# A fused encoder layer: the first input tile and the first weight tile loaded in halves, the norm weight alone in front of them

## The chip, the cores and the metric

The kernel runs on one core of a Trainium2 chip. The metric is the device time of one execution in microseconds; of several executions the median is given. A profile is one further execution recorded by the hardware profiler. Its times are counted from the first instruction, and its span is the time from the first to the last instruction.

## The reference

One layer of a hybrid encoder on an input of 512 positions by 1024 channels, in float32. The input is normalised, and one projection makes the inputs of three token mixers and the logits of three branch gates:

```python
h = rms_norm(x, norm_mix[l])                      # x * rsqrt(mean(x*x) + EPS) * g
proj = jnp.einsum('bsd,dc->bsc', h, w_in[l])      # 1024 -> 8192 columns
u_pool, u_lru, q, k, v, g_logits = jnp.split(proj, splits, axis=-1)
gates = jax.nn.sigmoid(g_logits + b_gate[l]).reshape(B, S, N_BRANCH, D_MODEL)
...
merged = (gates[:, :, 0] * (y_pool @ w_branch[l, 0])
          + gates[:, :, 1] * (y_lru @ w_branch[l, 1])
          + gates[:, :, 2] * (y_sb @ w_branch[l, 2]))
x = x + merged @ w_out[l]
h2 = rms_norm(x, norm_ffn[l])
x = x + (silu(h2 @ w_ffn_gate[l]) * (h2 @ w_ffn_up[l])) @ w_ffn_down[l]
```

`y_pool` comes from causal means over 2, 4, 8 and 16 positions, `y_lru` from a short convolution and a gated linear recurrence, `y_sb` from causal stick-breaking attention with 8 heads of 128. Of all this the change touches only the first step: the products of `norm_mix * x` with the first 512 gate columns of `w_in` (columns 5120 to 5631). The factor `rsqrt(mean(x*x) + EPS)` depends on the position alone and is multiplied in later.

## The kernel before, in words

**Precision.** Every operand of a large product is split into a high part, rounded to the matrix format (`fp32r`), and a low part, what the rounding left. A product then takes three matrix products: high by high, low weight by high input, high weight by low input. In the code `wh`/`wl` or `hi0`/`lo0` are the parts of a weight tile and `hh`/`hl` those of an input tile.

**Layout.** Channels lie on the 128 partitions, positions along the free dimension. The transposed input `xt` has 8 tiles of 128 x 512, numbered k. The small vectors of the layer (norm weights, biases, convolution taps, 114 columns in all) are packed in one array `vecs`, which a single transfer loads into the tile `vt` (L447). `vcol(name, i)` (L294) picks a column of it.

**The first stage.** Before any data is there, TensorE runs `WARM` = 9 products of a constant tile into a scratch bank (L421). Then the first four output tiles of the gate projection (4 x 128 columns, four accumulators) are computed k by k (L696): for each k, 4 products of `wh` by `hh`, 4 of `wl` by `hh`, 4 of `wh` by `hl`, each over 512 positions, 12 products a k and 96 in all. The weights come in chunks of two k (`("first", 0)` to `("first", 3)`). The first chunk is loaded and split by hand at L443 to L453: a transfer for each k, then a cast to `hi0` and a subtraction to `lo0` on VectorE. Later chunks go through `add_direct` and `split_w`: a transfer of 512 KB on SP (L117), the high part on ScalarE (L110), the low part on VectorE (L111). `make_h` (L433) makes `hh` of an input tile on ScalarE (L437: times the norm weight of that k) and `hl` on VectorE (L438). At k = 3 the loads and squares for the mean square are emitted (`input_rms`, L474).

**What sets the order.** Transfers are issued from SP's queue, in this stage also one from ScalarE's, and software transfers from POOL's. A planner assigns each engine its instruction order from the dependences, its own cost estimates and the order of the text; `tc.high_priority` moves blocks forward. So the order of the text is not always the order on the engine: the constants of the recurrence (`lru_constants`, L539 to L560: `qg`, the `lt` chain, `cpos`, `cneg`), which the text emits after the first chunks of the projection, run on VectorE as soon as `vt` is there. POOL computes one power of that chain (L547). Tiles have fixed places in SBUF; `pad` (L299, `PAD` columns) shifts what is allocated behind it.

**After it** come the other gate columns, the recurrence, the attention, the branch and output projections and the feed-forward network. From the attention projections on, many products are arranged as a seven-product scheme over halves of 256 columns (`product`, L282).

Of the kernel before, what the change touches and what calls it, by code (L numbers as in the profile page):

```python
# [8 lines left out]
F32 = mybir.dt.float32  # L9
F32R = mybir.dt.float32r  # L10
BF16 = mybir.dt.bfloat16
AF = mybir.ActivationFunctionType
ALU = mybir.AluOpType
# [3 lines left out]
P = 128  # L17
S = 512
D = 1024
KT = D // P  # L20
# [4 lines left out]
HD = 128  # L25
QSCALE = float(HD) ** -0.5
EARLY = 300
WARM = 9
GBUFS = 27
NDIRECT = 2  # L30
KD = 8
H = S // 2
AHEAD = 200
PAD = 41


OFF = 16
# [11 lines left out]
VOFF = {}  # L49
# [17 lines left out]
def layer_kernel(ctx: ExitStack, tc: tile.TileContext, x, xt, vecs, w_in, w_qkv7, w_gate7, w_pool, w_rg, w_ig,  # L67
                 w_branch, w_br7, w_out, w_fg, w_fu, w_fd, w_fd7, out):
    nc = tc.nc
    act = nc.scalar.activation  # L70
    dve = nc.vector

    cst = ctx.enter_context(tc.tile_pool(name="cst", bufs=1))
# [18 lines left out]
    def cols(ap, k0, nk, c0, nc_):  # L92
        return ap[k0 * P:(k0 + nk) * P, c0:c0 + nc_].rearrange("(k p) c -> p k c", p=P)
# [200 lines left out]
    def vcol(name, i=0):  # L294
        o = VOFF[name] + i
        return vt[:, o:o + 1]


    cst.tile([P, PAD], F32, tag="pad", name="pad")  # L299
    warm = cst.tile([P, S], BF16, tag="warm", name="warm")  # L300
    dve.memset(warm, 1.0)
# [106 lines left out]
    with ExitStack() as first:  # L408
# [18 lines left out]
        xts = [xp[k // 2][:, k % 2, :] for k in range(KT)]  # L427
        hu = []

        def load_xt(k):  # L430
            nc.sync.dma_start(xts[k], xt[k * P:(k + 1) * P, :])

        def make_h(k):  # L433
            t = t4([2, S], f"hu{k}", F32R)
            hh, hl = t[:, 0, :], t[:, 1, :]
            gcol = vcol("norm_mix", k)
            act(hh, xts[k], AF.Copy, scale=gcol)  # L437
            dve.scalar_tensor_tensor(hl, xts[k], gcol, hh.bitcast(F32), ALU.mult, ALU.subtract)  # L438
            hu.append((hh, hl))


# [1 line left out]
        hi0, lo0 = (t.rearrange("p (a b) -> p a b", a=2) for t in weight_tiles("whi0", "wlo0"))  # L443
        raw0 = wp.tile([P, 2, 512], F32, tag="raw", name="raw0")
        ready["first", 0] = hi0, lo0
        src0 = cols(w_in, 0, 2, 5120, 512)
        nc.sync.dma_start(vt, vecs)  # L447
        for k in range(2):
            load_xt(k)
            (nc.sync if k else nc.scalar).dma_start(raw0[:, k, :], src0[:, k, :])  # L450
            dve.tensor_copy(hi0[:, k, :], raw0[:, k, :])
            dve.tensor_tensor(lo0[:, k, :], raw0[:, k, :], hi0[:, k, :].bitcast(F32), ALU.subtract)
            make_h(k)  # L453
        load_xt(2)
        emit_next()
        make_h(2)
# [238 lines left out]
        pss = [chunk_psum(("gate", 0, c), pb) for c in range(2)]  # L695
        for k in range(KT):  # L696
            if k % 2 == 0:
                wh, wl = weights("first", k // 2)
            for w, x_ in ((wh, 0), (wl, 0), (wh, 1)):
                for n in range(4):  # L700
                    nc.tensor.matmul(pss[n // 2][n % 2], w[:, k % 2, n * P:(n + 1) * P], hu[k][x_],  # L701
                                     start=k == 0 and w is wh and x_ == 0,
                                     stop=k == KT - 1 and x_ == 1)
            if k == 3:
                input_rms()
        bg.append(rms_broadcast)
# [146 lines left out]
        for cc in range(2):  # L853
# [14 lines left out]
            for nm in ORDER:  # L868
                ps, half, first_, t, ts_, src, ss = plan[nm]
# [314 lines left out]
    with ExitStack() as third:  # L1184
# [42 lines left out]
        for u, nm in BORDER:  # L1227
            z, half, first_, sn, ts_ = plan[nm]
# [5 lines left out]
            for w in range(2):  # L1234
                o = ps[:, w, half * H:(half + 1) * H]
                for k in range(4):
                    for n, (x_, y_) in enumerate(((0, 0), (0, 1), (1, 0))):
                        nc.tensor.matmul(o, ah[x_][:, w, k, :], b[k][y_], start=first_ and n == k == 0,  # L1238
                                         stop=n == 2 and k == 3, skip_group_check=True)
            if sn is not None:  # L1240
                if (u, sn) not in snaps:
                    snaps[u, sn] = ap2.tile([P, 2, S], F32, tag="t", name=f"bt{u}{sn}")
                with tc.high_priority(EARLY):
                    act(snaps[u, sn][:, :, ts_], ps[:, :, hi], AF.Copy,
                        scale=-1.0 if sn and (u, sn) in gated else 1.0)
# [10 lines left out]
    with ExitStack() as ffn:  # L1256
# [18 lines left out]
        for c in range(4):  # L1275
# [7 lines left out]
            pss = psh[c] if c < 2 else chan_chunk(("out", c), mt, pool=fp)  # L1283
            hh = g4([2, S], f"h2h{c}", F32R)
            hl = g4([2, S], f"h2l{c}", F32R)
            for j in range(2):
                k = 2 * c + j
# [382 lines left out]
```

## Time and profile before

| what | value |
|---|---|
| median of 3 runs | 901.01 us (900.60 to 901.17) |
| the profiled execution | 900.73 us |
| its span | 899.0 us |
| TensorE busy | 893.4 us, 99% of the span |
| VectorE busy | 732.3 us, 81% |
| ScalarE busy | 523.2 us, 58% |
| granted clock of TensorE, mean | 1.000 |

In the rows of the profile PE is TensorE, PEld its weight loads, DVE VectorE, ACT ScalarE, POOL GpSimd, SP SyncE; a q behind the name is the engine's queue, where transfers are issued. A timeline row has start, length, engine, line, operation, output<-inputs and shape, and a count where neighbouring instructions are merged; in brackets stands how long the engine had been idle before and what ended that. The line is that of the kernel's source.

### The profile page before, as it was taken

The page shows a single profiled execution, that of the slowest core. Times are in us where ns is not written, and L with a number is a line of the kernel's source. Part 1 is how long each engine was busy: PE and PEld are TensorE (multiplying, and loading weights), DVE is VectorE, ACT ScalarE, POOL GpSimd, SP SyncE. Part 2 cuts the span into 40 slices and gives each one's busy share as a digit, 9 for nine tenths or more (in the row PEclk, how much of TensorE's full clock was granted, in tenths as well). Part 3 has the DMA queues.
Part 4 walks back from the last instruction along what each step waited for, and adds up shares of the span by engine and source line. Part 5 has one row for each costly group of instructions (what it writes and reads, how often), then busy time and mean ns, then how long its engine had stood idle before and what let it go on. Part 6 is the DMA issues. An engine that isn't in the chain of part 4 may idle for free.

```text
span 899.0 us, 14052 instructions
## 1 busy us (share of the span) xinstructions
PE 893.4 (99%) x5491; PEld 794.2 (88%) x5491; DVE 732.3 (81%) x922; ACT 523.2 (58%) x722; POOL 86.3 (10%) x126
## 2 busy tenths in 40 slices
PE   9999999999999999999999999999999999999998
PEld 6888778788899888888888988889999999989998
DVE  7897897988786599967887696699888888799764
ACT  7554989556856556555664544454555555664532
POOL 1110002232332101000001100000000000101200
PEclk9999999999999999999999999999999999999999
DMA  9585347789682785734736865245543333866842
GB/s 337 147 303 156 115 127 215 234 286 242 181 260 71 233 235 190 220 118 141 223 91 152 184 177 170 94 131 152 141 117 95 111 102 125 225 167 122 180 99 94
DMA packets 116579, 151.98 MB, mean 169 GB/s; under 512 B 8096, under 2 KB 90016, under 8 KB 116512
## 3 DMA queue, kind: packets, MB, share of 16 engines
q1 hardware_dynamic: 104416, 107.30, 37.7%
q0 software_dynamic: 11952, 43.52, 20.6%
q8 instruction: 43, 0.70, 0.3%
q10 hardware_dynamic: 144, 0.26, 0.1%
q14 instruction: 24, 0.20, 0.1%
HBM read 130.61 MB, written 18.87 MB: 166 GB/s over the span
## 4 chain that ended last, share of the span: by engine, by line
PE 95%; DVE 2%; ACT 2%; issue 1%; DMA 0%; SPq 0%; DVEq 0%; ACTq 0%
PE ps_y L287 11%; PE ps_x L287 8%; PE ps_q L798 7%; PE ps_dy L287 5%; PE ps_dx L287 4%; PE ps_br L278 3%; PE ps_br L279 3%; PE ps_br L280 3%; PE ps_gate L701 2%; PE ps_bY L1238 2%; PE ps_gy L287 2%; PE ps_gate L280 2%; PE ps_bX L1238 2%; PE ps_gx L287 2%; PE ps_gate L279 2%; PE ps_gate L278 2%
## 5 line engine op out<-in xcount | busy, mean ns | idle before, releaser
L110 ACT ACTIVATE whi<-raw 128x1024 fp32r<-128x1024 f32 x73 | 77.2, 1058 | 85.3 <-PE ps_out L279 17.0
L111 DVE TENSOR_TENSOR wlo<-raw,whi 128x1024 fp32r<-128x1024 f32 x73 | 89.1, 1220 | 32.9 <-ACT whi L110 32.9
L111 DVE TENSOR_TENSOR wlo<-qw,whi 128x1024 fp32r<-128x1024 f32 x48 | 58.6, 1222 | 20.8 <-ACT whi L110 20.5
L110 ACT ACTIVATE whi<-qw 128x1024 fp32r<-128x1024 f32 x48 | 50.8, 1057 | 33.1 <-PE ps_q L798 18.6
L1403 ACT ACTIVATE wh_S<-w_S 128x1024 fp32r<-128x1024 f32 x36 | 38.2, 1064 | 35.5 <-PE ps_y L287 22.4
L1404 DVE TENSOR_TENSOR wl_S<-w_S,wh_S 128x1024 fp32r<-128x1024 f32 x36 | 43.8, 1220 | 6.2 <-ACT wh_S L1403 6.2
L1403 ACT ACTIVATE wh<-w 128x1024 fp32r<-128x1024 f32 x27 | 28.8, 1066 | 30.3 <-issue 11.9
L1494 POOL DMA_DIRECT2D dw<-in_w_down_dram x16 | 13.5, 846 | 325.9 <-DVE wl L1404 248.2
L1404 DVE TENSOR_TENSOR wl<-w,wh 128x1024 fp32r<-128x1024 f32 x27 | 32.9, 1220 | 10.0 <-ACT wh L1403 10.0
L1403 ACT ACTIVATE whdS<-dw 128x1024 fp32r<-128x1024 f32 x16 | 17.0, 1064 | 24.4 <-PE ps_dy L287 13.2
L1404 DVE TENSOR_TENSOR wldS<-dw,whdS 128x1024 fp32r<-128x1024 f32 x16 | 19.6, 1224 | 12.9 <-ACT whdS L1403 12.9
L1054 DVE TENSOR_TENSOR_SCAN E<-K,ahead 128x512 f32<-128x512 f32 (+3 forms) x32 | 25.3, 812 | 4.4 <-ACT K L1050 4.4
L278 PE MATMUL ps_br<-yHH,whi 128*128 128x512 f32 x64 | 25.3, 395 | 0.0
L278 PE MATMUL ps_lru<-HH,whi 128*128 128x512 f32 x64 | 25.2, 394 | 0.0
L278 PE MATMUL ps_br<-yph,whi 128*128 128x512 f32 x64 | 25.2, 394 | 0.0
L278 PE MATMUL ps_pool<-HH,whi 128*128 128x512 f32 x64 | 25.2, 393 | 0.0
L279 PE MATMUL ps_br<-ypl,whi 128*128 128x512 f32 x64 | 25.0, 391 | 0.0
L280 PE MATMUL ps_gate<-HH,wlo 128*128 128x512 f32 x64 | 25.0, 391 | 0.0
L278 PE MATMUL ps_gate<-HH,whi 128*128 128x512 f32 x64 | 25.0, 391 | 0.0
L280 PE MATMUL ps_br<-yph,wlo 128*128 128x512 f32 x64 | 25.0, 391 | 0.0
L279 PE MATMUL ps_br<-yHL,whi 128*128 128x512 f32 x64 | 25.0, 390 | 0.0
L279 PE MATMUL ps_pool<-HL,whi 128*128 128x512 f32 x64 | 25.0, 390 | 0.0
(717 smaller groups left out, 3426.3 us busy)
## 6 DMA issues: line engine op xcount, KB each, us to landing
raw<-in_w_in_dram SPq DMA_DIRECT2D x31, 512.0 KB, 5.2
qw<-in_w_qkv_dram SPq DMA_DIRECT2D x24, 512.0 KB, 6.8
w<-in_w_ffn_gate_dram SPq DMA_DIRECT2D x36, 256.0 KB, 4.1
w<-in_w_ffn_up_dram SPq DMA_DIRECT2D x36, 256.0 KB, 4.6
raw<-in_w_branch_dram SPq DMA_DIRECT2D x16, 512.0 KB, 4.4
dw<-in_w_down_dram POOLq DMA_DIRECT2D x16, 512.0 KB, 6.3
qw<-in_w_qkv_dram POOLq DMA_DIRECT2D x12, 512.0 KB, 7.6
qd<-r POOLq DMA_DIRECT2D x12, 512.0 KB, 7.2
```

Source lines behind the costliest of these rows:

```text
L110: act(hi, raw, AF.Copy)
L111: dve.tensor_tensor(lo, raw, hi.bitcast(F32), ALU.subtract)
L278: nc.tensor.matmul(ps, lh, rh, start=start, stop=False, skip_group_check=skip)
L279: nc.tensor.matmul(ps, lh, rl, start=False, stop=False, skip_group_check=skip)
L280: nc.tensor.matmul(ps, ll, rh, start=False, stop=stop, skip_group_check=skip)
L287: nc.tensor.matmul(o, a_[a][:, w, k, :], b_[b][:, k, :], start=first and n == k == 0, stop=last and n == 2 and k == 3, skip_group_check=True)
L701: nc.tensor.matmul(pss[n // 2][n % 2], w[:, k % 2, n * P:(n + 1) * P], hu[k][x_], start=k == 0 and w is wh and x_ == 0, stop=k == KT - 1 a ...
L798: nc.tensor.matmul(ps[:, a, :], b_[:, k, ts_], a_[:, kk, :], start=first and n == k == 0, stop=n == 2 and k == 3, skip_group_check=True)
L1054: dve.tensor_tensor_scan(E[:, c0:c0 + n][:, ::-1], K[:, c0 + 1:c0 + n + 1][:, ::-1], ahead[:, S - n:][:, ::-1], 0.0, ALU.mult, ALU.add)
L1238: nc.tensor.matmul(o, ah[x_][:, w, k, :], b[k][y_], start=first_ and n == k == 0, stop=n == 2 and k == 3, skip_group_check=True)
L1403: act(h, src, AF.Copy)
L1404: dve.tensor_tensor(l, src, h.bitcast(F32), ALU.subtract)
```

## The change

- The norm weight's 8 columns get a tile of their own, `nmix`, loaded from `vecs` as the first transfer on SP; `make_h` takes its column from there. The pad shrinks from 41 to 33 columns.
- The first input tile is loaded as two transfers of 256 positions, the first on SP, the second on ScalarE's queue. The k = 0 part of the first weight tile is loaded as two transfers of 256 columns, the first on ScalarE's queue, the second on SP. The input tile of k = 1 and the k = 1 weight part follow on SP, and `vt` behind them.
- For k = 0, `hi0` and `lo0` are made in halves of 256 columns, and `hh` and `hl` in halves of 256 positions: both `hh` halves, then both `hl` halves.
- For k = 0 the products run in four groups: output tiles 0 and 1 with the first half of the positions, 0 and 1 with the second, 2 and 3 with the first, 2 and 3 with the second. Each group has 6 products of 256 positions, so 24 stand where 12 of 512 stood.
- `WARM` goes from 9 to 7.

```diff
-WARM = 9
+WARM = 7
-PAD = 41
+PAD = 33
...
+    nmix = cst.tile([P, 8], F32, tag="nmix", name="nmix")
...
-        def make_h(k):
+        def make_h(k, parts=(slice(0, S),)):
             t = t4([2, S], f"hu{k}", F32R)
             hh, hl = t[:, 0, :], t[:, 1, :]
-            gcol = vcol("norm_mix", k)
-            act(hh, xts[k], AF.Copy, scale=gcol)
-            dve.scalar_tensor_tensor(hl, xts[k], gcol, hh.bitcast(F32), ALU.mult, ALU.subtract)
+            gcol = nmix[:, k:k + 1]
+            for ts_ in parts:
+                act(hh[:, ts_], xts[k][:, ts_], AF.Copy, scale=gcol)
+            for ts_ in parts:
+                dve.scalar_tensor_tensor(hl[:, ts_], xts[k][:, ts_], gcol, hh[:, ts_].bitcast(F32),
+                                         ALU.mult, ALU.subtract)
             hu.append((hh, hl))
...
+        o = VOFF["norm_mix"]
+        nc.sync.dma_start(nmix, vecs[:, o:o + 8])
+
+        def round_first(k, cs):
+            dve.tensor_copy(hi0[:, k, cs], raw0[:, k, cs])
+            dve.tensor_tensor(lo0[:, k, cs], raw0[:, k, cs], hi0[:, k, cs].bitcast(F32), ALU.subtract)
+
+        HF = (slice(0, S // 2), slice(S // 2, S))
+        nc.scalar.dma_start(raw0[:, 0, HF[0]], src0[:, 0, HF[0]])
+        nc.sync.dma_start(xts[0][:, HF[0]], xt[0:P, HF[0]])
+        nc.scalar.dma_start(xts[0][:, HF[1]], xt[0:P, HF[1]])
+        nc.sync.dma_start(raw0[:, 0, HF[1]], src0[:, 0, HF[1]])
+        load_xt(1)
+        nc.sync.dma_start(raw0[:, 1, :], src0[:, 1, :])
+        for cs in HF:
+            round_first(0, cs)
+        make_h(0, HF)
+        round_first(1, slice(0, S))
+        make_h(1)
         nc.sync.dma_start(vt, vecs)
-        for k in range(2):
-            load_xt(k)
-            (nc.sync if k else nc.scalar).dma_start(raw0[:, k, :], src0[:, k, :])
-            dve.tensor_copy(hi0[:, k, :], raw0[:, k, :])
-            dve.tensor_tensor(lo0[:, k, :], raw0[:, k, :], hi0[:, k, :].bitcast(F32), ALU.subtract)
-            make_h(k)
...
-            for w, x_ in ((wh, 0), (wl, 0), (wh, 1)):
-                for n in range(4):
-                    nc.tensor.matmul(pss[n // 2][n % 2], w[:, k % 2, n * P:(n + 1) * P], hu[k][x_],
-                                     start=k == 0 and w is wh and x_ == 0,
-                                     stop=k == KT - 1 and x_ == 1)
+            for ns, ts_ in [(ns, ts_) for ns in ((0, 1), (2, 3)) for ts_ in HF] if k == 0 else \
+                    (((0, 1, 2, 3), slice(0, S)),):
+                for w, x_ in ((wh, 0), (wl, 0), (wh, 1)):
+                    for n in ns:
+                        nc.tensor.matmul(pss[n // 2][n % 2][:, ts_], w[:, k % 2, n * P:(n + 1) * P],
+                                         hu[k][x_][:, ts_],
+                                         start=k == 0 and w is wh and x_ == 0 and ts_ == HF[0],
+                                         stop=k == KT - 1 and x_ == 1, skip_group_check=True)
```

## The prediction

> **What bounds the kernel now.** I read the page's first part, then the chain of waits over the first 40 us, then the list of TensorE's own waits, and last the timelines of the first 12 us, engine by engine. The page says how much there is to win at all:
>
> ```profile
> span 899.0 us, 14052 instructions
> PE 893.4 (99%) x5491; PEld 794.2 (88%) x5491; DVE 732.3 (81%) x922; ACT 523.2 (58%) x722; POOL 86.3 (10%) x126
> ```
>
> TensorE is busy in all but 899.0 - 893.4 = 5.6 us of the span. The chain of waits in order of time (start, length, what) shows where a part of that lies:
>
> ```profile
> 0.74 0.39 SPq L447
> 1.19 3.35 DMA xt<-in_xt_dram
> 4.62 0.73 ACT hu L437
> 5.39 22.10 PE ps_gate L701 x96
> 27.49 0.23 PE ps_gate L278
> ```
>
> Behind the start stands one transfer (the first input tile), one activation that makes `hh` of it, and then 96 products without a break: 22.10 / 96 = 0.230 us each. So the first product starts at 5.39 and everything after it hangs on TensorE. TensorE's waits (engine, line, who ended it: total, times, longest):
>
> ```profile
> PE warm_ps L422 <- DVE warm L301: 1.5, 1, 1.5
> PE ps_gate L701 <- ACT hu L437: 0.5, 1, 0.5
> PE ps_q L798 <- DVE wlo L111: 0.4, 1, 0.4
> ```
>
> The third comes much later, and there are no others. A product begun earlier therefore moves the end by nearly as much, provided that the next tiles keep up.
>
> **What feeds the first products.** Transfers issued around 1.2 us, with the time from issue to landing; the second raw half of the first weight tile; the next weight chunk (512 KB); and a transfer with rows of 32 bytes:
>
> ```profile
> raw<-in_w_in_dram ACTq DMA_DIRECT2D x1, 256.0 KB, 3.1
> xt<-in_xt_dram SPq DMA_DIRECT2D x1, 256.0 KB, 3.3
> vt<-in_vecs_dram SPq DMA_DIRECT2D x1, 57.0 KB, 2.9
> ```
> ```profile
> raw<-in_w_in_dram SPq DMA_DIRECT2D x1, 256.0 KB, 4.5
> bigx<-in_vecs_dram SPq DMA_DIRECT2D x2, 2.0 KB, 6.8
> ```
> ```profile
> raw<-in_w_in_dram SPq DMA_DIRECT2D x1, 512.0 KB, 5.9
> ```
>
> SP's issues of interest (start, length over all, count), and what the transfer engines did, in windows whose last two columns are their busy share and GB/s:
>
> ```profile
> 1.19 0.90 SPq L431 DMA_DIRECT2D xt<-in_xt_dram  x2
> 2.12 0.43 SPq L450 DMA_DIRECT2D raw<-in_w_in_dram  x1
> 3.07 0.56 SPq L117 DMA_DIRECT2D raw<-in_w_in_dram  x1
> ```
> ```profile
> 0.00:5.00 5.00, 3.41 (x9) 1.14 (x9) 1.82 (x7) 1.97 (x3) 2.24 (x26) 1.00 0.66 189
> 5.00:10.00 5.00, 4.61 (x20) 3.79 (x21) 3.87 (x9) 2.77 (x5) 0.94 (x1) 1.00 0.98 352
> ```
>
> `vt` lands at 0.74 + 2.9 = 3.6, the raw tile at 0.74 + 3.1 = 3.85, the input tile at 1.19 + 3.35 = 4.53, the second raw part at 2.12 + 4.5 = 6.63, the next chunk at 3.07 + 5.9 = 9.0. From 5 us on the transfer engines are full (0.98), so from there landings follow the bytes ahead of them, not the moment of issue.
>
> ScalarE and VectorE in the same stretch:
>
> ```profile
> 4.62 1.53 ACT L437 ACTIVATE hu<-xt,vt 128x512 fp32r<-128x512 f32 x2 [1.85 <-DMA xt<-in_xt_dram]
> 9.02 1.06 ACT L110 ACTIVATE whi<-raw 128x1024 fp32r<-128x1024 f32 x1 [0.78 <-DMA raw<-in_w_in_dram]
> ```
> ```profile
> 3.63 0.15 DVE L540 TENSOR_SCALAR qg<-vt 128x1 f32<-128x1 f32 x1 [2.23 <-DMA vt<-in_vecs_dram]
> 3.70 0.16 DVE L544 TENSOR_SCALAR lt<-vt 128x8 f32<-128x8 f32 x1
> 3.90 0.17 DVE L545 TENSOR_TENSOR lt<-lt,vt 128x8 f32<-128x8 f32 x1
> 3.98 0.42 DVE L451 CAST whi<-raw 128x512 fp32r<-128x512 f32 x1
> 4.32 0.17 DVE L557 TENSOR_SCALAR lt<-lt 128x8 f32<-128x8 f32 x1
> 4.44 0.69 DVE L452 TENSOR_TENSOR wlo<-raw,whi 128x512 fp32r<-128x512 f32 x1
> 5.38 1.56 DVE L438 SCALAR_TENSOR_TENSOR hu<-xt,vt,hu 128x512 fp32r<-128x512 f32 x2 [0.25 <-ACT hu L437]
> 6.85 0.42 DVE L451 CAST whi<-raw 128x512 fp32r<-128x512 f32 x1
> 7.30 0.69 DVE L452 TENSOR_TENSOR wlo<-raw,whi 128x512 fp32r<-128x512 f32 x1
> 8.28 0.75 DVE L438 SCALAR_TENSOR_TENSOR hu<-xt,vt,hu 128x512 fp32r<-128x512 f32 x1 [0.28 <-ACT hu L437]
> 10.12 1.23 DVE L111 TENSOR_TENSOR wlo<-raw,whi 128x1024 fp32r<-128x1024 f32 x1 [0.56 <-ACT whi L110]
> ```
>
> TensorE's row that holds the last four products of k=0 and the first four of k=1:
>
> ```profile
> 7.37 1.99 PE L701 MATMUL ps_gate<-hu,whi 128*128 128x512 f32 x8
> ```
>
> Two margins decide what an early start is worth. Products of k=1 begin at 7.37 + 4 x 0.23 = 8.28 and need `hi` of k=1, ready at 6.85 + 0.42 = 7.27: margin 1.0. The `lo` products of k=2 begin 12 + 4 products later, at 11.95, and need `lo` of the next chunk, ready at 10.12 + 1.23 = 11.35: margin 0.6. That chunk lands when it lands, so **no early start is worth more than about 0.6 us** unless its transfer comes earlier too.
>
> **The change part by part.**
>
> *Halves on TensorE.* 24 products of 256 columns stand where 12 of 512 stood. One window of a later stage has nothing but 256-column products, and their halves on the other engines are there too (last columns: busy total, mean ns):
>
> ```profile
> 645.00:655.00 10.00, 10.00 (x91) 10.00 (x90) 1.00 0.57 160
> ```
> ```profile
> L1336 DVE SCALAR_TENSOR_TENSOR hn<-x,vt,rb 128x256 f32<-128x256 f32 x16 | 6.5, 479 | 0.0
> ```
> ```profile
> L1094 ACT ACTIVATE B34h<-ysb 128x256 fp32r<-128x256 f32 x8 | 3.2, 414 | 4.4 <-DVE ysb L1121 3.5 <-DVE vl L1029 0.9
> ```
>
> 10.00 / 91 = 0.11 us a product, half of 0.23: the halves cost nothing on TensorE (0.00), although each loads its weights again.
>
> *The first input half.* On SP stand `nmix` (0.74), then the first half of the input (1.18); the other half goes from ScalarE's queue. `nmix` is 4 KB in 128 rows, as many rows as `vt` and in its place; I price its landing as `vt`'s, 3.6 (the 32-byte rows of `bigx` took 6.8, but behind a full queue). The half has 128 KB: it lands no sooner than `vt`'s 2.9 us after issue, 4.08, and no later than the whole one, 4.53. Ahead of it or beside it stand some 260 to 390 KB instead of 57 + 512, so I take 4.15. The half activation: 0.41 (the 256-column row) to 0.72; I take 0.45. First product: 4.15 + 0.08 + 0.45 + 0.04 = 4.7, **0.7 earlier**.
>
> *Fewer warm products (seven for nine).* They hold TensorE's queue until the row below ends; without them it would be
>
> ```profile
> 1.46 3.41 PE L422 MATMUL warm_ps<-warm 128*128 128x512 bf16 x9 [1.46 <-DVE warm L301]
> ```
> ```profile
> 4.00 0.88 PE L422 MATMUL warm_ps<-warm 128*128 128x512 bf16 x3
> ```
>
> free of the seventh at about 4.3 (six take (4.00 - 1.46) / 6 = 0.42 each, the last three about 0.25), ahead of 4.7. Nine would end at 4.87 and eat 0.1 to 0.2 of the gain.
>
> *VectorE's order.* In the text it is now: cast and subtract of the first weight half, cast and subtract of the second, then `hl` of the two input halves. Half of 0.42 is 0.21 as a floor, I take 0.25; half of 0.69 I take as 0.38; `hl` as 0.45 (the 256-column row has 0.48). The second weight half stands behind 516 KB instead of 569 KB for 4.53: 4.5 with its shorter rows. So: cast 4.55 to 4.8, subtract to 5.2, `hl` of the first half to 5.65, of the second to 6.1. TensorE has four products ready at 4.7 (0.45 us), wants `hl` at 5.15 and gets it at 5.7: a stall of 0.55. Then 20 products at 0.113 (between the 0.11 of the window and half of 0.23): k=1 begins at 5.7 + 2.26 = 7.95 against 8.28, **0.33 earlier**. If the planner puts `hl` of the first half before the second cast, the wait moves to `hl` of the second half (wanted 5.82, there 6.1) and k=1 begins at 7.7, 0.55 earlier: just inside the margin. Both are later than 7.27, so `hi` of k=1 is there; its cast starts after `hl` of k=1, at 6.1 + 0.75 = 6.85, as before.
>
> *SP's queue.* `nmix`, one more half of the weights and `vt` move about; the next chunk is issued two places later, 2 x (2.12 - 1.19) / 2 = 0.93 us, at 4.0. It still waits behind full transfer engines, and the bytes ahead of it grow by 4 KB, so it lands at 9.0; were this cover gone, it would land 0.93 late and wipe out the gain. Shorter rows: zero to 0.2 us on the same landing; I take none, since the share of the engines that is not yet used before 5 us (0.66) takes them.
>
> *Constants behind.* `vt` stands behind the second raw part and lands at about 6.8 (57 KB more than that part's 6.63). Waiting for it: `qg` and the `lt` chain, needed tens of microseconds later, and POOL's power, which sits on an idle engine. Cost none where the planner puts them late. The new small tile and the smaller pad sum to the same 41 columns: none.
>
> **Sum**: 900.73 (the profiled execution, 1.7 over its span) - 0.35 = 900.4. That execution lies 0.28 under the median of 901.01, so for a median I say 900.6.
>
> [...] The last three warm products run at nearly twice the pace of the first six. [...]
>
> **The rivals.**
> 1. *`vt` holds VectorE.* On VectorE `qg` and `lt` stood ahead of the first cast. If they still do, the first cast waits for 6.8 instead of 3.85: cast at 7.2, first product 7.5, `hl` of the first half 8.9, k=1 at 8.9 + 2.3 = 11.2 against 8.28: +2.9, giving 903.6 to 903.9. It decides from the place where they precede the second cast; behind `hl` of the second half they cost some 0.7 and the gain turns to +0.3. For it: rows 3.63 to 3.90. Against: that order came with `vt` landing first, and now it is loaded eighth.
> 2. *A later order changes.* The planner reorders work far from the start; TensorE's other waits are so short that a new one can only add. Two or three of the size of the largest in the list (0.5 to 1.5) give 901.5 to 903.5. Nothing in the profile shows it; the reverse, a gain over 1.8, exceeds both the margin of 0.6 and the 1.5 us between 3.9 (a half that lands as early as the raw tile) and 5.39.
> 3. *The gain does not arrive.* The chunk of 9.0 lands later, or the clock comes as late as nine slow warm products last (1.46 + 9 x 0.42 = 5.25), so that the products between 4.7 and 5.25 do half their work: 0.0 to 0.1 left, 900.7 to 901.0.
>
> **Numbers.** Forecast (gain of 0.1 to 0.6) 0.6; no gain or a loss under 1.8 us, from rivals 1 to 3, 0.16; slower by more, 0.10 from the first rival and 0.08 from the second; faster by more 0.06, for a changed order that helps. 0.2% is 1.8 us, about what a measurement of this kernel tells from no change. Faster 0.06, same 0.76, slower 0.18. The likeliest case alone spans 900.1 to 900.9. The range goes from 899.9 (first product at 4.2, all of it kept) up into the first two rivals, to 902.8, which leaves out the worst form of both.
>
> **What would show it.** First `ps_gate` product at 4.7 with `hh` in two halves before it; a wait of TensorE on `hl` of about half a microsecond behind the fourth product; k=1 at 7.7 to 8.0; the `lo` of the second chunk still at about 11.4, and `ps_gate` L278 at 27.1 instead of 27.49. I am wrong if `qg` precedes the weight casts on VectorE, if the chunk of 9.0 lands later than 9.2, or if TensorE's list of waits gains rows after 28 us.

## The result and the profile after

The changed kernel takes **902.85 us** (median of 22 executions, 902.48 to 903.48). The kernel before, run beside it on the same chip, takes 901.19 us (22 executions, 900.53 to 902.34). The ratio is 1.0018, interval 1.0011 to 1.0024: about 1.7 us slower, where the forecast was 0.4 us faster. It is a small loss, 0.2% of the time, but the interval leaves out 1. The profiled execution of the changed kernel took 902.55 us; its page says:

```profile
span 900.8 us, 14081 instructions
PE 894.5 (99%) x5501; PEld 794.7 (88%) x5501; DVE 732.7 (81%) x925; ACT 524.7 (58%) x723; POOL 86.3 (10%) x126
```

TensorE is idle 6.3 us, against 5.6 before. The chain of waits in order of time (start, length, what) has changed its shape:

```profile
2.13 3.77 DMA xt<-in_xt_dram
5.93 0.74 ACT hu L441
6.69 0.75 DVE hu L443
7.44 0.34 DVE whi L457
7.92 0.59 DVE wlo L458
8.75 1.69 POOL lt L567
11.79 1.24 DVE wlo L111
13.08 15.72 PE ps_gate L724 x68
28.80 0.23 PE ps_gate L278
```

Before, the chain was one input tile, one activation and 96 products on end. Now only 68 of the stage's 108 products are on it. Ahead of these stand the low half of the second weight chunk (`wlo`, L111), a power on POOL, VectorE's work on k = 1, and at the start the input tile of k = 1 (issued at 2.13). The product that follows the first stage (first row of L278) starts at 28.80 against 27.49: **1.31 us of the loss lie in the first 13 us.** What follows that row takes 902.55 - 28.80 = 873.75 us; before it took 873.24, and over all the kernels below it takes 873.1 to 874.0. So that row can stand for the head of the kernel, and a difference of some tenths behind it is scatter. TensorE's waits (who ended it: total, times, longest) name the places:

```profile
PE warm_ps L425 <- DVE warm L304: 1.5, 1, 1.5
PE ps_gate L724 <- DVE wlo L111: 0.6, 1, 0.6
PE ps_q L822 <- DVE wlo L111: 0.4, 1, 0.4
PE ps_gate L724 <- ACT whi L110: 0.3, 1, 0.3
```

The second and the fourth are new, and both belong to the second chunk. TensorE's timeline shows that the early start arrived and was then lost:

```profile
4.48 0.79 PE L724 MATMUL ps_gate<-hu,whi 128*128 128x256 f32 x2
5.08 0.46 PE L724 MATMUL ps_gate<-hu,wlo 128*128 128x256 f32 x2
...
7.61 0.40 PE L724 MATMUL ps_gate<-hu,wlo 128*128 128x256 f32 x2
7.85 1.33 PE L724 MATMUL ps_gate<-hu,whi 128*128 128x256 f32 x6
9.02 1.07 PE L724 MATMUL ps_gate<-hu,wlo 128*128 128x512 f32 x4
9.93 1.07 PE L724 MATMUL ps_gate<-hu,whi 128*128 128x512 f32 x4
11.28 1.20 PE L724 MATMUL ps_gate<-hu,whi 128*128 128x512 f32 x4 [0.28 <-ACT whi L110]
13.08 1.19 PE L724 MATMUL ps_gate<-hu,wlo 128*128 128x512 f32 x4 [0.60 <-DVE wlo L111]
```

The first product starts at 4.48 instead of 5.39, 0.91 us earlier. At 11.28 the high half of the second chunk holds TensorE, at 13.08 the low half. Before, the `lo` products of that chunk started at 11.92:

```profile
11.92 1.07 PE L701 MATMUL ps_gate<-hu,wlo 128*128 128x512 f32 x4
```

Why they are late stands in the rows of SP's issues, of ScalarE and of VectorE:

```profile
3.08 0.43 SPq L473 DMA_DIRECT2D vt<-in_vecs_dram  x1
3.56 0.43 SPq L434 DMA_DIRECT2D xt<-in_xt_dram  x1
4.03 0.43 SPq L117 DMA_DIRECT2D raw<-in_w_in_dram  x1
```
```profile
10.17 1.06 ACT L110 ACTIVATE whi<-raw 128x1024 fp32r<-128x1024 f32 x1 [0.60 <-DMA raw<-in_w_in_dram]
```
```profile
7.70 0.15 DVE L560 TENSOR_SCALAR qg<-vt 128x1 f32<-128x1 f32 x1
...
10.46 0.17 DVE L568 TENSOR_SCALAR lt<-lt 128x8 f32<-128x8 f32 x1
...
11.71 0.17 DVE L575 TENSOR_SCALAR lt<-lt 128x8 f32<-128x8 f32 x1
11.79 1.23 DVE L111 TENSOR_TENSOR wlo<-raw,whi 128x1024 fp32r<-128x1024 f32 x1
```

Two delays, one of the transfer and one of the order on VectorE. The chunk is issued at 4.03 (before: 3.07) and lands at 10.14, just ahead of the cast at 10.17 (before: 9.0 and 9.02). Its high half is ready at 10.17 + 1.06 = 11.23, but its low half does not start there: VectorE first runs seven instructions of the recurrence's constants (10.46 to 11.79), which had waited for POOL's power. So `lo` is ready at 11.79 + 1.23 = 13.02, against 11.35 before.

### The profile page after: what moved, and what is told of

Its sections match the earlier page's. It is cut to its first block, busy times and chain, and to the rows that moved or that the text cites. A ratio compares the mean times of both kernels' runs of the same rounds, so it can differ in the third digit from the quotient of the medians.

```text
span 900.8 us, 14081 instructions
## 1 busy us (share of the span) xinstructions
PE 894.5 (99%) x5501; PEld 794.7 (88%) x5501; DVE 732.7 (81%) x925; ACT 524.7 (58%) x723; POOL 86.3 (10%) x126
## 4 chain that ended last, share of the span: by engine, by line
PE 94%; DVE 3%; ACT 2%; issue 1%; DMA 0%; POOL 0%; SPq 0%; DVEq 0%; POOLq 0%
PE ps_y L287 11%; PE ps_x L287 8%; PE ps_q L822 7%; PE ps_dy L287 5%; PE ps_dx L287 4%; PE ps_br L278 3%; PE ps_br L279 3%; PE ps_br L280 3%; PE ps_bY L1262 2%; PE ps_gy L287 2%; PE ps_gate L280 2%; PE ps_bX L1262 2%; PE ps_gx L287 2%; PE ps_gate L278 2%; PE ps_gate L279 2%; PE ps_gate L724 2%
## 5 line engine op out<-in xcount | busy, mean ns | idle before, releaser
L111 DVE TENSOR_TENSOR wlo<-raw,whi 128x1024 fp32r<-128x1024 f32 x73 | 89.2, 1222 | 33.3 <-ACT whi L110 33.3
L111 DVE TENSOR_TENSOR wlo<-qw,whi 128x1024 fp32r<-128x1024 f32 x48 | 58.7, 1224 | 20.8 <-ACT whi L110 20.5
L278 PE MATMUL ps_br<-yHH,whi 128*128 128x512 f32 x64 | 25.3, 395 | 0.0
L278 PE MATMUL ps_lru<-HH,whi 128*128 128x512 f32 x64 | 25.2, 394 | 0.0
L278 PE MATMUL ps_br<-yph,whi 128*128 128x512 f32 x64 | 25.2, 394 | 0.0
L278 PE MATMUL ps_pool<-HH,whi 128*128 128x512 f32 x64 | 25.2, 394 | 0.0
L278 PE MATMUL ps_gate<-HH,whi 128*128 128x512 f32 x64 | 25.0, 391 | 0.0
L280 PE MATMUL ps_pool<-HH,wlo 128*128 128x512 f32 x64 | 25.0, 391 | 0.0
```

Of the source, the lines that this page charges most:

```text
L111: dve.tensor_tensor(lo, raw, hi.bitcast(F32), ALU.subtract)
L278: nc.tensor.matmul(ps, lh, rh, start=start, stop=False, skip_group_check=skip)
L280: nc.tensor.matmul(ps, ll, rh, start=False, stop=stop, skip_group_check=skip)
```

## The experiments

The theories have letters. **A**: the row constants (`qg` and the `lt` chain), which now come late with `vt`, stand on VectorE ahead of the second chunk's `lo`. **B**: that chunk is issued two places later on SP and lands later by as much. **C**: the halves' shorter rows make the transfers slower wherever they are issued. **D**: the halves on the engines cost something themselves. Times before stand beside each run, since each was measured with runs of the kernel before on the same chip. Where the interval holds 1, the kernel's time is not told from that of the kernel before. The columns behind the interval are of one profiled execution each; "k = 1" is the start of the first product of k = 1, and "full speed" the moment at which the record of TensorE's clock reaches full speed (last section).

| kernel | median us (range, n) | before | ratio (interval) | chunk issued, landed | `lo` starts | full speed | k = 1 | first L278 |
|---|---|---|---|---|---|---|---|---|
| before, as shown | | | | 3.07, 9.00 | 10.12 | 4.11 | 8.29 | 27.49 |
| after, as shown | 902.85 (902.48 to 903.48, 22) | 901.19 | 1.0018 (1.0011 to 1.0024) | 4.03, 10.14 | 11.79 | 5.19 | 8.09 | 28.80 |
| constants_behind | 901.80 (901.17 to 902.07, 11) | 901.22 | 1.0005 (0.9996 to 1.0014) | 4.03, 10.20 | 11.32 | 6.02 | 8.23 | 28.31 |
| vt_late | 901.56 (901.23 to 902.36, 11) | 901.22 | 1.0005 (0.9996 to 1.0014) | 3.55, 9.57 | 10.69 | 5.17 | 8.61 | 27.94 |
| halves_on_engines_only | 901.19 (900.56 to 901.82, 11) | 901.22 | 0.9999 (0.9990 to 1.0008) | 3.07, 9.00 | 10.12 | 6.21 | 8.73 | 27.96 |
| norm_weight_only | 901.72 (901.11 to 902.82, 11) | 901.22 | 1.0006 (0.9997 to 1.0015) | 3.63, 9.13 | 11.66 | 5.96 | 8.41 | 28.65 |
| two_more_issues | 902.17 (900.88 to 902.38, 11) | 901.10 | 1.0008 (0.9999 to 1.0017) | 4.23, 9.50 | 11.01 | 7.15 | 9.28 | 28.48 |
| act_takes_half | 903.71 (901.63 to 905.75, 9) | 901.10 | 1.0024 (1.0014 to 1.0034) | 3.08, 8.95 | 10.06 | 10.70 | 10.74 | 29.99 |
| whole_tiles | 900.74 (900.30 to 901.36, 11) | 901.10 | 0.9995 (0.9986 to 1.0004) | 3.07, 8.98 | 10.11 | 5.78 | 8.37 | 27.60 |
| split_by_rows | 903.97 (902.49 to 905.05, 6) | 901.10 | 1.0032 (1.0020 to 1.0044) | 4.06, 10.43 | 11.55 | 5.03 | 9.35 | 28.83 |
| input_halves | 901.35 (900.65 to 901.95, 12) | 901.20 | 0.9996 (0.9988 to 1.0005) | 3.08, 9.81 | 10.93 | 6.80 | 8.79 | 28.02 |
| before_warm_7 | 901.66 (900.58 to 903.21, 12) | 901.20 | 1.0002 (0.9992 to 1.0012) | 3.07, 9.31 | 10.43 | 9.38 | 10.13 | 29.36 |

Two things are read from these columns below. From the start of k = 1 to the first L278 row it is 19.2 to 19.5 us in before and in most kernels, whether the chunk lands early or late; only the change (20.7), constants_behind (20.1) and norm_weight_only (20.2) take clearly longer, and there TensorE waits for the second chunk. What the other kernels lose, they lose ahead of k = 1. And landings scatter: four profiles in which SP issues the same transfers as in before (both of before, halves_on_engines_only, before_warm_7) have the chunk at 8.83 to 9.31, so a difference of less than about 0.5 us between two single profiles decides nothing.

**The constants behind the second chunk's `lo`** (the changed kernel with nothing else moved; `ins` is the subtraction of that chunk):

```diff
         def lru_constants():
-            dve.tensor_scalar(qg, vcol("q_norm"), QSCALE, None, ALU.mult)
+            with tc.issue_after(second[0]):
+                dve.tensor_scalar(qg, vcol("q_norm"), QSCALE, None, ALU.mult)
...
+        if n == "1":
+            second.append(ins.ins)
```

> The changed kernel with one edit: the constants of the recurrence (qg and the lt chain) are queued on VectorE behind the subtraction that makes lo of the second weight chunk; all transfers as in the changed kernel. In the changed kernel that subtraction starts at 11.79 although its high part is done at 11.23, with ten small constant instructions ahead of it that wait for POOL's power (until 10.44). Theory A (the late vt pushes the constants between): the subtraction starts at about 11.25, TensorE's wait for it shrinks by 0.55 us, the time falls from 902.85 to about 902.3. Theory B (all of the loss is the chunk's late landing): no change, 902.85. The chunk lands at 10.1 by both.

901.80, so the order of these small instructions is worth 1.05 us of the 1.66; the two kernels' executions do not overlap (902.48 and more against 902.07 and less). The rows of ScalarE and VectorE show the low half directly behind the high half (10.23 + 1.06 = 11.29), although the chunk lands no earlier:

```profile
10.23 1.06 ACT L112 ACTIVATE whi<-raw 128x1024 fp32r<-128x1024 f32 x1 [1.30 <-DMA raw<-in_w_in_dram]
```
```profile
11.32 1.23 DVE L113 TENSOR_TENSOR wlo<-raw,whi 128x1024 fp32r<-128x1024 f32 x1 [1.60 <-ACT whi L112]
```

A holds, and is larger than expected. In the profile shown above, `lo` could have started 0.04 behind its high half, as in before, and the constants held it for only 11.79 - 11.27 = 0.52. The second profile of the changed kernel, below, shows why the median has more.

**`vt` behind the third chunk's place** (the changed kernel with one issue moved; the constants then come late by themselves, and the second chunk is issued one place earlier):

```diff
         make_h(1)
-        nc.sync.dma_start(vt, vecs)
         load_xt(2)
...
         emit_next()
+        nc.sync.dma_start(vt, vecs)
         make_h(4)
```

> The changed kernel with vt loaded only behind the transfer of the third weight chunk. That takes the constants off VectorE's queue ahead of the second chunk and moves that chunk's issue on SP one place up (3.55 instead of 4.03). Theory A alone: landing still 10.1, time 902.3. Theory B (the landing follows SP's place in the queue): landing 9.65, high part done 10.75, low part 12.0 instead of 13.0; with A together the time falls by about 1.0 to 901.85. Theory C (halved rows slow the transfer engines whatever the order): landing 10.0 (57 KB less ahead of it), time 902.15.

901.56, nearer to B's value than to C's. The chunk is issued 0.48 us earlier than in the change and lands 0.57 earlier; `lo` starts at 10.69, as early as its high half allows, still 0.57 later than before. But the time does not speak for B, since TensorE no longer waits for this chunk: its `lo` is ready at 10.69 + 1.23 = 11.92, and the products that take it start at 12.34. TensorE's only new wait, 0.49 ahead of k = 1, is for the high half of the k = 1 weights (first row); on VectorE (second and third) `hl` of k = 1 stands ahead of that cast:

```profile
PE ps_gate L724 <- DVE whi L457: 0.5, 1, 0.5
```
```profile
7.38 0.75 DVE L443 SCALAR_TENSOR_TENSOR hu<-xt,nmix,hu 128x512 fp32r<-128x512 f32 x1 [1.23 <-ACT hu L441]
8.04 0.42 DVE L457 CAST whi<-raw 128x512 fp32r<-128x512 f32 x1
```

The input tile of k = 1 landed at 6.60 here, at 5.40 before: it is issued one place later, too. So a first product 0.94 us earlier (4.45) ends in a k = 1 that is 0.3 later (8.61 against 8.29).

**Halves on the engines only** (the kernel before; casts, activations and products of k = 0 by halves as in the change, all transfers whole and in their old order):

```diff
+            for ts_ in parts:
+                act(hh[:, ts_], xts[k][:, ts_], AF.Copy, scale=gcol)
...
+            for cs in HF if k == 0 else (slice(0, S),):
+                round_first(k, cs)
```

> The kernel before with its whole transfers and vt in front, but casts, subtractions, input halves and products of k = 0 by halves as in the changed kernel. Theory D (halved products or halved casts cost by themselves): later than 901.2 by 0.5 us or more. Theories A, B and C: the chunk lands at 9.0 as before, the first product starts 0.2 earlier (its activation is half as long), and the time is 900.9 to 901.3, no different from before.

901.19 against 901.22, so D's 0.5 us or more is not seen (the interval goes from 0.9 us faster to 0.7 slower). The row of L278 is 0.47 late in this profile, but that is the clock: full speed came at 6.21, and the four products ahead of it took 0.94. The other 20 took 2.40, 0.12 each, where half of 0.227 would make 2.27: 0.13 us on these may be the halves'.

**The norm weight alone in front, `vt` behind k = 1, nothing halved** (the kernel before):

```diff
+        o = VOFF["norm_mix"]
+        nc.sync.dma_start(nmix, vecs[:, o:o + 8])
-        nc.sync.dma_start(vt, vecs)
         for k in range(2):
...
+        nc.sync.dma_start(vt, vecs)
         load_xt(2)
```

> The kernel before with the norm weight alone in front and vt behind the k = 1 weight part; nothing is halved, nine warm products. The chunk is issued one place later. Theory A: the constants stand ahead of the second chunk's low part and wait for vt (about 7.2) and POOL's power (about 10.4), the low part starts at about 11.6 instead of 10.1, TensorE waits 0.9 us more: 902.0. Theory B: landing 9.5, low part about 11.9 if nothing stands ahead of it, wanted at 11.9: 901.2. Theory C (halves slow the transfers): landing 9.0, 901.2.

901.72, 0.5 over the kernel before, which the interval does not tell from nothing; but TensorE's list of waits has the row of the change again, without any half:

```profile
PE ps_gate L704 <- DVE wlo L111: 0.7, 1, 0.7
```

The constants run at 10.53 to 11.66 ahead of `lo`, whose high half was ready at 9.15 + 1.06 = 10.21. That is A by itself: with a chunk that lands in time, `lo` is as late as in the change (11.66 against 11.79). B is not seen here: the chunk is issued 0.56 us later and lands only 0.13 later.

**Two more issues ahead of the chunk** (the kernel before; two transfers of 4 KB into the pad, which nothing reads):

```diff
             load_xt(k)
+            nc.sync.dma_start(padt[:, 8 * k:8 * k + 8], vecs[:, 8 * k:8 * k + 8])
```

> The kernel before with two transfers of 4 KB more on SP (into the unused pad tile), so that the second weight chunk is issued at 4.0 instead of 3.07, as late as in the changed kernel, with the same large transfers and rows. The planner also puts eight small constant instructions ahead of that chunk's low part, but with vt in front they are done before 10. Theory B (landing follows the place in SP's queue): landing 9.9, low part 12.2, TensorE waits 0.3 us: 901.5. Theory C (the halved transfers slow the engines; the place does not matter): landing 9.0 to 9.2 and 901.2.

902.17. The chunk is issued 1.16 later and lands 0.50 later: with whole tiles less than half of the delay arrives. None of the loss comes from that: `lo` is ready at 11.01 + 1.22 = 12.23, ahead of the products that take it (12.91), although the constants stand ahead of it here too. The 0.99 by which L278 is late is there at k = 1 (9.28 against 8.29). The first product is 0.48 late (5.87, the input tile landed later), and full speed came at 7.15. So this run says something of the landing, and nothing of what a late landing costs.

**What the transfer engines did** says how far B and C can be told apart. In windows (the last two columns are the engines' busy share and GB/s), first the changed kernel, then the kernel before:

```profile
0.00:2.50 2.50, 1.04 (x3) 0.43 (x4) 0.48 (x1) 0.83 (x1) 1.47 (x25) 1.00 0.20 55
2.50:5.00 2.50, 2.50 (x7) 0.97 (x6) 0.88 (x3) 1.67 (x4) 0.00 (x0) 1.00 0.89 260
5.00:7.50 2.50, 2.45 (x20) 2.24 (x19) 2.08 (x6) 0.73 (x1) 0.00 (x0) 1.00 0.93 293
```
```profile
0.00:2.50 2.50, 1.04 (x3) 0.44 (x4) 0.48 (x1) 1.32 (x2) 1.46 (x25) 1.00 0.26 33
2.50:5.00 2.50, 2.37 (x7) 0.71 (x5) 1.33 (x6) 0.65 (x2) 0.78 (x1) 1.00 1.06 346
5.00:7.50 2.50, 2.10 (x9) 1.74 (x10) 2.17 (x5) 1.07 (x2) 0.94 (x1) 1.00 0.96 343
```

By 7.5 us the changed kernel has moved 2.5 x (55 + 260 + 293) = 1520 KB, the kernel before 2.5 x (33 + 346 + 343) = 1805 KB: 285 KB behind, which at before's 343 GB/s is 0.83 us of the 1.14 that the chunk lands later. From 2.5 us on the engines were busy for 0.89 and 0.93 of the time, against 1.06 and 0.96 before, and carried less for it. The same sum gives 1485 KB for vt_late, 1757 for norm_weight_only, 1625 for two_more_issues, 1787 for whole_tiles and 1865 for halves_on_engines_only. In the change SP starts one transfer each 0.47 us whatever its size: with halves that is 128 KB / 0.47 = 272 GB/s on this queue, with whole tiles twice that. It is not shown that the engines ran short of work by this: up to 2.61 us SP and ScalarE had issued 4 + 4 x 128 + 2 x 256 = 1028 KB, and by 5.0 only 2.5 x (55 + 260) = 787 KB had moved. The short rows have a price in the trace's records of single rows: a row of 1 KB holds one of the 16 engines for 46 ns (median), one of 2 KB for 84. So the 512 short rows in place of 256 long ones cost (512 x 46 - 256 x 84) / 16 = 128 ns, 0.13 us of the 1.14. The long rows, too, took more in the mean, 119 ns from 2.5 to 5 us and 101 from 5 to 7.5, against 98 and 91 before, with the same median; why is open.

**The second weight half on ScalarE's queue** (vt_late with that one transfer moved, so that the chunk is issued at 3.08 with all halves kept):

```diff
-        nc.sync.dma_start(raw0[:, 0, HF[1]], src0[:, 0, HF[1]])
+        nc.scalar.dma_start(raw0[:, 0, HF[1]], src0[:, 0, HF[1]])
```

> vt_late with the second half of the first weight part issued from ScalarE's queue instead of SP's, so that the second chunk is issued at 3.08, as in the kernel before, while the halves stay. Theory B: landing 9.1, low part 11.4, TensorE starts 0.9 earlier and loses 0.3 to it: 900.7. Theory C: landing 9.6 as in vt_late (it is issued 0.47 earlier there for nothing), time as vt_late, 901.5.

On the landing this is B's value: with all the shorter rows, but issued in its old place, the chunk lands at 8.95 (1780 KB moved by 7.5 us). That speaks against C alone. In the kernels with both tiles in halves of columns the chunk lands 5.8 to 6.2 us behind its issue in all five profiles, as B has it; with the input tile alone in halves (below) it is 6.7. But the time is 903.71, a miss. The moved half was the third transfer on ScalarE's queue and landed at 5.74 instead of 4.70 (vt_late); TensorE stood 0.17 us for it (second row), and then ran at half pace:

```profile
5.31 0.63 PE L724 MATMUL ps_gate<-hu,wlo 128*128 128x256 f32 x2
6.11 0.80 PE L724 MATMUL ps_gate<-hu,whi 128*128 128x256 f32 x2 [0.17 <-DVE whi L457]
...
9.06 1.05 PE L724 MATMUL ps_gate<-hu,whi 128*128 128x256 f32 x4
9.91 0.63 PE L724 MATMUL ps_gate<-hu,wlo 128*128 128x256 f32 x2
10.34 1.49 PE L724 MATMUL ps_gate<-hu,whi 128*128 128x256 f32 x6
```

From 9.06 to 9.91 four products of 256 columns take 0.85, 0.21 each, where the changed kernel has 0.12 (two in the 0.24 from 7.61 to 7.85). Its clock rose at 10.70 only, and that is most of the loss: the 24 products of k = 0 took 10.74 - 4.72 = 6.0 us instead of 24 x 0.12 = 2.9. More on that below.

**Halves by rows instead of columns** (vt_late; each half is 64 partitions of full 2 KB rows, so that no row is shorter):

```diff
-        nc.sync.dma_start(xts[0][:, HF[0]], xt[0:P, HF[0]])
-        nc.scalar.dma_start(xts[0][:, HF[1]], xt[0:P, HF[1]])
+        nc.sync.dma_start(xts[0][PH[0], :], xt[PH[0], :])
+        nc.scalar.dma_start(xts[0][PH[1], :], xt[PH[1], :])
```

> vt_late with the first input tile and the first weight part loaded in two transfers of 64 partitions and whole 2 KB rows instead of two of 128 partitions and 1 KB rows; as many transfers and bytes, in the same places. The first product then needs both transfers of the input tile. Theory C1 (short rows cost): the second chunk lands at 9.1 instead of 9.6. Theory C2 (the number of transfers costs): it lands at 9.6 again. First product at about 4.7 and the time 901.2 by C1, 901.6 by C2.

903.97: worse still. The chunk lands at 10.43, later than by C1 and by C2, so whole rows gave nothing back, but its issue moved as well, to 4.06: SP needs 0.56 and 0.58 us for the two issues of 64 partitions instead of 0.43 (and 0.58 for the whole tile behind them). The second part of the input lands at 5.44, and the products of both halves need both parts:

```profile
PE ps_gate L725 <- ACT hu L441: 1.5, 1, 1.5
```

The profiled execution is the fastest of the six (902.49). What made the median 1.5 us longer still is in no profile.

**Whole tiles, norm weight in front, `vt` late** (vt_late with the first tiles loaded whole and nine warm products; the halves on the engines stay):

```diff
-WARM = 7
+WARM = 9
...
-        nc.scalar.dma_start(raw0[:, 0, HF[0]], src0[:, 0, HF[0]])
-        nc.sync.dma_start(xts[0][:, HF[0]], xt[0:P, HF[0]])
-        nc.scalar.dma_start(xts[0][:, HF[1]], xt[0:P, HF[1]])
-        nc.sync.dma_start(raw0[:, 0, HF[1]], src0[:, 0, HF[1]])
+        for k in range(2):
+            load_xt(k)
+            (nc.sync if k else nc.scalar).dma_start(raw0[:, k, :], src0[:, k, :])
```

> The norm weight alone in front and vt behind the third chunk, all transfers whole, casts, input halves and products of k = 0 by halves, nine warm products: the parts of the change without its halved transfers. Theory C: landing of the second chunk 9.0, first product at 5.0 (input tile 0.15 earlier, first activation 0.2 shorter), nothing in front of the low part, which is done at 11.35 against 11.55 wanted: 900.8, 0.4 faster than before. If the halves of transfers are what starts TensorE early and nothing else counts: 901.2.

900.74, the lowest median of all: 2.1 us under the change. Against the kernel before, the ratio 0.9995 has 1 in its interval, so it is not shown to be faster. The chunk is back at 8.98 and `lo` at 10.11; the first product starts at 5.08, and the chain now puts the warm products in front of it and no transfer (it counts them to 5.48, since ends of products are modelled and overlap the next):

```profile
1.46 4.02 PE warm_ps L425 x9
5.48 22.12 PE ps_gate L719 x108
```

**The input tile alone in halves** (whole_tiles with seven warm products and two transfers for the input tile):

```diff
+        nc.sync.dma_start(xts[0][:, HF[0]], xt[0:P, HF[0]])
+        nc.scalar.dma_start(xts[0][:, HF[1]], xt[0:P, HF[1]])
```

> The kernel of whole_tiles, but the input tile of k=0 in two halves, the first on SP's queue and the second on ScalarE's behind the weight tile, which stays whole; seven warm products; the row constants behind the third chunk as there. If the early start counts in full (the forecast's mechanism): the second chunk is issued at about 3.1 and lands at 9.0, the first product starts at about 4.6 instead of 5.08, and the time is 0.4 under whole_tiles, 900.3. If the moment of the full clock decides, products ahead of it count half: 0.2 at most is left, 900.5. [...]

Neither came: the median, 901.35, lies 0.6 over that of whole_tiles instead of 0.2 to 0.4 under it. The half on SP lands at 1.19 + 3.20 = 4.39, where it landed at 3.83 in the change (there 128 KB of weights went beside it, here 256 KB, which may be why), so the first product starts at 5.05, no earlier than with a whole tile. The chunk, issued at 3.08, lands at 9.81; the last of its 16 shares came 0.96 us after the fifteenth. Why that one is late is not settled. It cost nothing: TensorE has no wait for the chunk, and k = 1 is already 0.42 later than in whole_tiles, with full speed at 6.80 instead of 5.78. The range, 900.65 to 901.95, is no wider than others.

**Seven warm products in the kernel before**:

```diff
-WARM = 9
+WARM = 7
```

> The kernel before with seven warm products instead of nine and nothing else. The first product waits for the input tile, so without the clock nothing changes: first product 5.4, 901.1, spread as before. [...]

The median moves little, 901.66, but the executions fall apart: six lie between 900.58 and 900.93, six between 902.38 and 903.21, and none between. The profile fell into the upper group (902.68):

```profile
5.47 2.08 PE L701 MATMUL ps_gate<-hu,whi 128*128 128x512 f32 x4 [0.84 <-ACT hu L437]
7.34 1.91 PE L701 MATMUL ps_gate<-hu,wlo 128*128 128x512 f32 x4
9.05 2.17 PE L701 MATMUL ps_gate<-hu,whi 128*128 128x512 f32 x8
11.06 1.07 PE L701 MATMUL ps_gate<-hu,wlo 128*128 128x512 f32 x4
```

Eight products from 5.47 to 9.05 take 0.45 each, eight from 9.05 to 11.06 take 0.25. The clock rose at 9.38. The middle of the upper group, 902.81, is 2.0 us over that of the lower, 900.82. This execution has a gap of 0.84 us ahead of the first product, and a late clock. But that seven warm products cause the two groups is not shown. The median is not told from that of the kernel before, and of the 23 executions of the kernel before that ran beside it five lie between 902.13 and 904.68; no execution of the lower group was profiled.

**A second profile of both kernels.**

> The kernel before, profiled a second time. By the theory of the issue's place the second chunk lands about 6 us behind its issue at 3.1, thus at 8.9 to 9.1, and its lo half starts at about 10.1 again. [...]

The chunk landed at 8.83, `lo` started at 9.95, and the clock rose at 4.11 as before: 901.22 us, first L278 at 27.23.

> The changed kernel, profiled a second time. By the theory of the constants the lo half of the second chunk starts at 11.8 again, behind the row constants, even if the chunk lands earlier than 10.1; by the theory that the late landing alone sets it, it moves with the landing. [...]

This execution (902.84 us) is the clearest case of A. The chunk lands at 9.87, earlier than in the first profile, and `lo` starts *later*, at 12.24. ScalarE's row, then VectorE's:

```profile
9.90 1.06 ACT L110 ACTIVATE whi<-raw 128x1024 fp32r<-128x1024 f32 x1 [0.76 <-DMA raw<-in_w_in_dram]
```
```profile
10.91 0.17 DVE L568 TENSOR_SCALAR lt<-lt 128x8 f32<-128x8 f32 x1 [0.96 <-POOL lt L567]
...
12.16 0.17 DVE L575 TENSOR_SCALAR lt<-lt 128x8 f32<-128x8 f32 x1
12.24 1.23 DVE L111 TENSOR_TENSOR wlo<-raw,whi 128x1024 fp32r<-128x1024 f32 x1
```

The high half was ready at 9.90 + 1.06 = 10.96; the constants hold `lo` for 12.24 - 11.0 = 1.24 here and for 0.52 in the first profile, around the 1.05 between the medians. They hang on the input tile of k = 1 (6.36 here, 5.90 there), since they are queued behind its work. The clock rose at 4.48, earlier than in the first profile (5.19), and did not help, because the constants set the time. That fits the narrow range of the changed kernel, 1.0 us against 1.8 before.

## Why the prediction was wrong

- **First product at 4.7**: right in kind; it was 4.48 and 4.52 (the input half landed at 3.83, not 4.15).
- **A wait of 0.55 for `hl` behind the fourth product**: 0.87 in the second profile, where the second weight half landed at 5.36 (forecast 4.5) and `hl` stood behind its cast. In the first profile hardly any wait shows, because the products started at half pace (the first two took 0.60, in the second profile 0.34) and filled the time until `hl` was there (5.05 + 0.48 = 5.53).
- **k = 1 at 7.7 to 8.0**: the row at 7.85 has two products of k = 0 and four of k = 1, so k = 1 started at about 7.85 + 2 x 0.12 = 8.1. The early start was 0.91 us, yet only some 0.2 of it reached k = 1, against a forecast of 0.33; in the second profile k = 1 came at 8.6, later than before (8.29). The slow clock ahead of 5.19, the third rival's, cost little here, as `hl` came at 5.53 in any case. From there the 20 products took 8.09 - 5.59 = 2.50 instead of 2.26.
- **Halves on TensorE: cost 0.00**: nearly right; 0.12 a product instead of 0.113, 0.13 us on 20 (halves_on_engines_only), and no difference in the median.
- **SP's queue, "lands at 9.0"**: this step failed. The text named the price of the other case, "were this cover gone, it would land 0.93 late and wipe out the gain", and that happened, with 1.14. The forecast counted bytes ahead of the chunk and took the engines as full; but by 7.5 us they had moved 285 KB less. Two terms priced at nothing stand behind it: the two later places, and the "shorter rows", 0.13 by the estimate above. The margin ahead of `lo` in before was 11.92 - 11.35 = 0.57.
- **Constants behind, "Cost none where the planner puts them late"**: this step failed too, and it is the larger term, 1.05 us by the medians. They did not go late: they went behind k = 1, and there they met the second chunk's `lo`. The first rival (`vt` holds VectorE) had the right mechanism at another place. It looked at the first cast and at `hl`, and not at the next instruction with little slack.
- **Rival 2**, a changed order far on: not seen; from L278 on the kernel takes 873.75 us against 873.24.
- **Rival 3**: its first form came, as the chunk landed at 10.14 instead of 9.0. Its second form, a clock that rises later than in the row of the warm products, was an assumption that no trace showed at the time; in the runs full speed began between 4.11 and 10.70 us, in the change at 5.19 and 4.48.

The sum was 0.35 us gained. In its place the first profile has `lo` ready 13.02 - 11.35 = 1.67 late; less the margin of 0.57, 1.10 is left, most of the 1.31 by which L278 moved, and the 0.2 gained at k = 1 goes into the wait. The two causes overlap and cannot simply be added. The constants alone would hold `lo` nearly as long: with the chunk in time norm_weight_only starts it at 11.66. The landing alone is constants_behind: 901.80, 0.58 over the kernel before, which its interval does not tell from nothing. And vt_late shows a third delay behind these two: the input tile of k = 1, issued one place later, made k = 1 itself late. The forecast had its work on VectorE "as before". What the runs don't separate is how the later landing divides between the issue's place and the lower rate of the engines; with whole tiles a later place cost 0.13 of 0.56 and 0.50 of 1.16, with both tiles in halves about all of it, each by one or two profiles.

## What to carry to other kernels

When a start is made earlier, write down for the next few tiles when each is *needed* and when each is *ready*, and check every engine queue in front of the tightest of them: here the margin was 0.57 us, and seven instructions on eight columns, delayed with their transfer, used it up. A transfer that is cut in halves costs a whole place in the queue for half the bytes (here 0.47 us on SP for 128 KB as for 256); ask what then lands later, the next input tile as well as the next weights, and not only how many bytes lie ahead. Small work that "can wait" must be told to wait: taken out of the way by an order it gave back 1.05 us, and by a later transfer, which also moved the chunk one place up, 1.29.

## What the runs showed of the hardware

**The moment at which the clock rises.** In the trace's record of the granted clock (which starts with full speed, so that the windows above print 1.00 for the time ahead of it, too), full speed begins at 4.11 (both profiles of before), 4.48, 5.03, 5.17, 5.19, 5.78, 5.96, 6.02, 6.21, 6.80, 7.15, 9.38 (before_warm_7) or 10.70 (act_takes_half). Products ahead of that moment take about twice as long (0.45 against 0.25 for 512 columns in before_warm_7, 0.21 against 0.12 for 256 in act_takes_half), so work that is moved ahead of it counts about half. The two latest moments are those of kernels in which TensorE stood shortly before or behind the first products (gaps of 0.84, and of 0.17 besides late weights). split_by_rows had a longer gap, 1.53, and its clock rose within it, at 5.03; so a gap does not always go with a late moment. What sets the moment is not shown: no run varied a gap alone. In before_warm_7 the eight slow products from 5.47 to 9.05 took 3.58 us, where eight at the 0.23 of the kernel before take 1.84: 1.7 us lost, near the 2.0 between its two groups. How many executions pay for fewer warm products the runs do not show.

**Places in the queue.** In the change an issue on SP takes 0.39 to 0.43 us up to 4.5 us, and the next follows 0.44 to 0.48 after it, for 4 KB as for 512 KB; single ones of other kernels took up to 0.58 (split_by_rows). A third transfer on ScalarE's queue (issued there at 1.66) landed at 5.74, where the same bytes, issued on SP at 1.66, landed at 4.70 to 5.36 in four profiles: another queue was not a faster one.
